# The third dense block's products in another order, and a head's norm spread half a piece later

## The chip, the cores and the metric

One core of a Trainium2 chip runs the whole program. The metric is the device time of one execution in microseconds. TensorE (PE) multiplies into PSUM banks of 128x512 floats; VectorE (DVE) and ScalarE (ACT) work on SBUF and PSUM; GpSimd (POOL) adds a little and issues transfers, SyncE (SP) issues most of them. Each engine runs its own instructions in program order and waits at semaphores for the others.

## The reference, cut to what matters

```python
for i in range(DEPTH):                       # two layers: gMLP mixer, then retention mixer
    h = rmsnorm(x, norm_mix_g[i])
    h = chunked_spatial_gating(h, ...) if i % 2 == 0 else retention(h, ...)
    x = x + h
    h = rmsnorm(x, norm_ffn_g[i])
    a = jax.nn.relu(h @ mlp_w1[i])           # 512 tokens x 4096 features
    x = x + (a * a) @ mlp_w2[i]
return rmsnorm(x, final_norm_g)
# retention, per head: o = rmsnorm(o, head_norm_g) * silu(g);  then  o @ w_out
```

The dense part of each layer and the head norm of the retention layer are what the change touches.

## The kernel before, in words

Every float32 product is three matmuls of float32r halves (`mm3`, L261): high by high, high by low, low by high. A weight piece is cast to its high half by ScalarE (L220) and its low half is taken by VectorE (L227, `tensor_sub`). The order of work is a list of steps written by hand; each step has one or two weight pieces. After a step's matmuls are issued, `refill` (L246) casts high halves up to three pieces ahead and takes low halves up to two pieces ahead. Matmuls of 512 columns go 24 to a piece (12 in each half of a product below).

**Dense layers.** `dense(l, hooks)` (L800) computes 4096 features in four groups of 1024: an up piece is 24 matmuls in a `mis` bank, and its evacuation is L695 (VectorE) and L696 (ScalarE). The second matrix product of the first three groups (blocks q = 0, 1, 2) is done by `seven(l, q)` (L719) with seven products of half-sized blocks, S0 to S6, in place of eight. Each product multiplies an operand of activations (`make(s)`: sums or differences of blocks by VectorE, their high halves by ScalarE in L763, their low halves by VectorE in L764) with a weight or a sum of weights. Operand s + 1 is made behind the first of product s's two pieces. `BANK = "acbacaa"` says which pair of PSUM banks (a, b or c) each product accumulates in: S0, S3, S5 and S6 use a, S1 and S4 use c, S2 uses b. After each product VectorE adds the pair's running sums to the token rows (L792), so the next product in the same pair waits for that.

The products alternate with up pieces, by a string of u and p. In blocks 0 and 1 every product is followed by an up piece. In the third block (q = 2) the string is `upupupupuupuupp`: its last two products stand next to each other. Just before the sixth product a `do` splits four chunks of activations of the last group into halves (`split_a`, L713 on ScalarE, L714 on VectorE), and four more behind it. Then comes the last quarter of the second matrix: in layer 0 `dn0` pieces (`down_last`, L836), in layer 1 `dt` pieces.

**Weights of the products.** Weight sums are formed by transfers: S5's weight is a load by SP (L165) followed by an accumulating load by POOL (L199, the add) into the same buffer, W12 + W22. S4's weight is W22 alone, a plain load. S1, S3 and S6 share one buffer to which further adds are applied once the earlier sum has been split. Loads take one of three rotating buffers as they come free, in the order of the steps.

**The head norm.** In the retention layer `o_unit(h)` (L1001) is the output product of head h: four pieces, each with two halves t of 12 matmuls, evacuated by L560. `finish_head(h + 1)` (L1010) hangs the next head's norm behind the pieces of `o_unit(h)`: behind piece 0 the sum of squares over the partitions, the reciprocal root and the two diagonal matrices `dg` (L340); behind piece 1 the two matmuls with ones that spread the row (`bc_h`, L344 and L345) and ScalarE's copy of it to SBUF (L346); behind pieces 2 and 3 `make_y` (L974 to L977), which scales the head and splits it into `ryH` and `ryL`. This is done for heads 1, 2 and 3; the third time, the product of head 3 follows at once and reads these halves. Head 0 has its norm elsewhere.

Of the kernel before, what the change touches and what calls it, by code (L numbers as in the profile page):

```python
# [88 lines left out]
def trunk(ctx, tc, x, norm_mix_g, norm_ffn_g, a_w_in, a_b_in, a_v_norm_g, a_w_s, a_b_s, a_w_out,  # L89
# [13 lines left out]
    def big(shape, dt, name):  # L103
        return bigp.tile(shape, dt, tag="big", name=name)

    def tmp(name, tag, bufs=2):
        return work.tile([P, T], F32, tag=tag, name=name, bufs=bufs)
# [7 lines left out]
    def acc(name):  # L115
        return psum.tile([P, 512], F32, tag="acc", name=name, bufs=6)
# [4 lines left out]
    def f32(ap):  # L121
        return ap.bitcast(F32)
# [110 lines left out]
    def launch(g):  # L233
        if next(g, "end") != "end":
            pending.append(g)

    def advance():
        for g in list(pending):
            if next(g, "end") == "end":
                pending.remove(g)  # L240
# [5 lines left out]
    def refill():  # L246
        n = pos["done"]
        prep(n + (LOOK if n >= 4 else 1), n + (LOOK - 1 if n >= 4 else 1))

    def step(fn, *ps):  # L250
        for p in ps:
            order.append(p)
            raws.extend(r for r in p.raws if r not in raws)
            for r in p.raws:
                r.uses += 1
        steps.append((fn, ps))
# [4 lines left out]
    def mm3(ps, ah, al, bh, bl, start, stop, resumed=False):  # L261

        for i, (a, b) in enumerate(((ah, bh), (ah, bl), (al, bh))):
            nc.tensor.matmul(ps, lhsT=a, rhs=b, start=start and i == 0, stop=stop and i == 2, skip_group_check=resumed)  # L264
# [96 lines left out]
    def mm_o(p, t, ps, bH, bL):  # L361
        ts = slice(t * P, (t + 1) * P)
        for k in range(4):
            mm3(ps, p.hi[:, k, ts], p.lo[:, k, ts], bH[:, k, :], bL[:, k, :], k == 0, k == 3)
# [187 lines left out]
    def evac_x(gcol=None, scaled=False):  # L552

        def ev(i, ps):
            if scaled:
                t = tmp(f"xs{i}", "uz")
                nc.vector.tensor_mul(t, ps, r2bc)
                nc.vector.tensor_add(xT[i], xT[i], t)
            else:
                nc.vector.tensor_add(xT[i], xT[i], ps)  # L560
            if gcol is not None:
                norm_chunk(i, gcol)
        return ev

    def out_piece(p, i, h, name, gcol=None, before=None, behind=None, act=None, bank=acc, scaled=False):

        ev = evac_x(gcol, scaled)
        hi, lo = act or (yH, yL)

        def run(p):  # L570
            if before:
                before()
            for t in range(2):
                ps = bank(f"{name}{h}_{i}{t}")
                mm_o(p, t, ps, hi[h], lo[h])
                if t == 1:
                    advance()
                    refill()
                    if behind:
                        behind()  # L580
                ev(2 * i + t, ps)
        step(run, p)

    def nxt(g, times=1):
        return lambda: [next(g, None) for _ in range(times)]
# [133 lines left out]
    def seven(l, q):  # L719

        w = mlp_w2[l]

        def part(i, j):
            r, c = 1024 * q + 512 * i, 512 * j
            return w[r : r + 512, c : c + 512].rearrange("(k p) n -> p k n", p=P)

        t1 = Raw(part(0, 0), adds=[part(0, 1)])
        t2 = Raw(part(1, 1), adds=[part(1, 1)], over=t1)
        t4 = Raw(part(1, 0), adds=[part(1, 0)], over=t2)
        wraws = [Raw(part(0, 0)), t1, Raw(part(1, 0)), t2, Raw(part(1, 1)), Raw(part(0, 1), adds=[part(1, 1)]), t4]  # L730
        pl = [[Piece(r, (slice(None), slice(2 * i, 2 * i + 2), slice(None)), [P, 2, 512]) for i in range(2)] for r in wraws]
        lo_t, hi_t = slice(0, T // 2), slice(T // 2, T)
        sums, parts, banks = {}, {}, {}

        def block(h, ts, c):
            return aF[2 * q + h][:, 2 * c : 2 * c + 2, ts]

        def half(v):
            return v.rearrange("p (k t) -> p k t", t=T // 2)

        def make(s):

            def src(c):
                if s in (0, 2, 6):
                    return block(*((0, lo_t), None, (1, lo_t), None, None, None, (1, hi_t))[s], c)
                if s == 1:
                    sums["s", c] = half(tmp(f"sa{l}{q}{c}", "uz"))
                    nc.vector.tensor_sub(out=sums["s", c], in0=block(0, hi_t, c), in1=block(1, hi_t, c))
                elif s == 3:
                    nc.vector.tensor_sub(out=sums["s", c], in0=sums["s", c], in1=block(0, lo_t, c))  # L750
                elif s == 4:
                    nc.vector.tensor_add(out=sums["s", c], in0=sums["s", c], in1=block(1, lo_t, c))
                else:
                    sums["d", c] = half(tmp(f"sd{l}{q}{c}", "sq"))
                    nc.vector.tensor_sub(out=sums["d", c], in0=block(0, lo_t, c), in1=block(0, hi_t, c))
                    return sums["d", c]
                return sums["s", c]

            sp = parts[s] = big([P, 2, 4, T // 2], F32R, f"sp{l}{q}{s}")
            for c in range(2):  # L760
                v = src(c)
                hi, lo = sp[:, 0, 2 * c : 2 * c + 2, :], sp[:, 1, 2 * c : 2 * c + 2, :]
                nc.scalar.copy(out=hi, in_=v)  # L763
                nc.vector.tensor_sub(out=lo, in0=v, in1=f32(hi))  # L764

        BANK = "acbacaa"
        FIRST = (0, 1, 2)
        OUT = [((0, 0), ALU.add), ((1, 1), ALU.add), ((0, 0), ALU.add), ((0, 1), ALU.subtract), ((0, 1), ALU.add), ((1, 1), ALU.subtract), ((1, 0), ALU.add)]

        def one(s, i):  # L770
            def run(p):
                bk = BANK[s]
                if i == 0 and s in FIRST:
                    banks[bk] = [acc(f"sm{l}{q}{bk}{t}") for t in range(2)]
                sp = parts[s]
                for t in range(2):
                    ts = slice(t * P, (t + 1) * P)
                    for k in range(2):
                        kk = 2 * i + k
                        mm3(banks[bk][t], sp[:, 0, kk, ts], sp[:, 1, kk, ts], p.hi[:, k, :], p.lo[:, k, :], s in FIRST and kk == 0, kk == 3, True)  # L780
                advance()
                refill()
                if i == 0 and s < 6:
                    make(s + 1)
                if i == 1:
                    (m, n), op = OUT[s]
                    for t in range(2):
                        v = tok[n][:, 2 * m + t, :]
                        if (n, m) in fresh:
                            nc.scalar.activation(v, banks[bk][t], AF.Copy, scale=1.0 if op == ALU.add else -1.0)  # L790
                        else:
                            nc.vector.tensor_tensor(out=v, in0=v, in1=banks[bk][t], op=op)  # L792
                    fresh.discard((n, m))
            return run

        return (lambda: make(0)), [lambda s=s: [step(one(s, i), pl[s][i]) for i in range(2)] for s in range(7)]

    fresh = set()

# [167 lines left out]
    def make_y(h, cs):  # L967
        if 0 in cs:
            yH[h] = big([P, 4, T], F32R, f"ryH{h}")
            yL[h] = big([P, 4, T], F32R, f"ryL{h}")  # L970

        def gen():
            for c in cs:
                nc.vector.tensor_mul(oo[h][:, c, :], oo[h][:, c, :], r2bc)  # L974
                nc.scalar.copy(out=yH[h][:, c, :], in_=oo[h][:, c, :])
            for c in cs:
                nc.vector.tensor_sub(out=yL[h][:, c, :], in0=oo[h][:, c, :], in1=f32(yH[h][:, c, :]))  # L977
            return
            yield
        launch(gen())  # L980
# [20 lines left out]
    def o_unit(h, gcol=None, behind=None):  # L1001
        behind = behind or {}
        pl = pieces_o(b_w_out[0], (h * DV, (h + 1) * DV), (0, D))
        for i in range(4):
            out_piece(pl[i], i, h, "ro", gcol, behind=behind.get(i))

    def each(fn, h):
        return {i: (lambda i=i: fn(h, i)) for i in range(4)}

    def finish_head(h):  # L1010
        g = head_norm(h)
        return {0: nxt(g, 3), 1: nxt(g), 2: lambda: make_y(h, (0, 1)), 3: lambda: make_y(h, (2, 3))}

    v_unit(0, {0: nxt(nrm1), 1: nxt(nrm1, 2), 3: nxt(nrm1)})
    do(trig_scaled)
# [123 lines left out]
    for k in range(2):  # L1139
        p = order[0]  # L1140
# [52 lines left out]
```

## Time and profile before

| | us |
|---|---|
| median of 3 runs | 1388.99 |
| lowest and highest run | 1388.95, 1390.54 |
| the profiled execution | 1390.09 |
| its span, first to last instruction | 1388.40 |
| TensorE busy in the span | 1367.0 (98%) |
| VectorE busy | 878.3 (63%) |
| ScalarE busy | 567.8 (41%) |
| mean granted TensorE clock | 0.994 |

A timeline row gives the start and the length in us, the engine (a q behind it means its queue), the line of the kernel, the operation, written and read tiles, shapes, how many instructions were merged in the row, and in brackets how long the engine sat idle before it and what ended that. A matmul's length counts its way through the pipeline; the next one starts before its end.

### The profile page before, as it was taken

The numbers are of one execution on the slowest core, as the hardware profiler recorded it, in microseconds if no ns is written. First come the engines' busy times: TensorE is split into PE (matmuls) and PEld (weight loads), VectorE is DVE, ScalarE is ACT, GpSimd is POOL, SyncE is SP. The second block draws the span as 40 slices with busy tenths as digits, with TensorE's granted clock in tenths as the row PEclk, the third lists the DMA queues.
The fourth block names the chain that finished last, engine by engine and source line by source line (L and its number), as shares of the span: only waits on it lengthen the run. The fifth ranks groups of instructions, "written<-read, shape, count | busy, mean of one in ns | idle before, by whom it ended". The sixth has DMA issues, their size and how long they took to land.

```text
span 1388.4 us, 15488 instructions
## 1 busy us (share of the span) xinstructions
PE 1367.0 (98%) x6180; PEld 1134.7 (82%) x6180; DVE 878.3 (63%) x1228; ACT 567.8 (41%) x812; POOL 158.0 (11%) x122
## 2 busy tenths in 40 slices
PE   9999999999999999999999999999999999999997
PEld 7888888888888888788888888888888888888875
DVE  7757756666656766676656574574594576657555
ACT  4646634234544443422333332323334444444342
POOL 3010111130100100021111100100121000100002
PEclk9999999999999999999999999999999999999999
DMA  6332222245665754623222222131137475765611
GB/s 229 110 117 81 75 89 92 91 144 155 148 191 152 183 144 130 165 84 99 84 70 81 70 95 87 61 122 61 61 95 209 93 187 175 152 182 152 172 56 61
DMA packets 115801, 166.71 MB, mean 120 GB/s; under 512 B 2881, under 2 KB 67985, under 8 KB 115473
## 3 DMA queue, kind: packets, MB, share of 16 engines
q1 hardware_dynamic: 103024, 140.55, 30.5%
q0 software_dynamic: 12672, 25.17, 10.7%
q8 instruction: 48, 0.79, 0.2%
q14 instruction: 25, 0.20, 0.0%
q10 hardware_dynamic: 32, 0.01, 0.0%
HBM read 163.62 MB, written 2.10 MB: 119 GB/s over the span
## 4 chain that ended last, share of the span: by engine, by line
PE 95%; DVE 3%; POOL 0%; ACT 0%; issue 0%; DMA 0%; SPq 0%; ACTq 0%; DVEq 0%
PE up L264 24%; PE g L264 6%; PE vv L264 6%; PE qk L264 6%; PE u L264 6%; PE o L264 6%; PE v L264 5%; PE ro L264 5%; PE dt L264 3%; PE dn L264 2%; PE av L264 2%; PE sm11a L264 2%; PE sm10a L264 2%; PE sm01a L264 2%; PE sm00a L264 2%; PE sm02a L264 2%
## 5 line engine op out<-in xcount | busy, mean ns | idle before, releaser
L227 DVE TENSOR_TENSOR wL<-raw,wH 128x1024 fp32r<-128x1024 f32 x235 | 300.6, 1282 | 56.1 <-issue 17.9
L220 ACT CAST wH<-raw 128x1024 fp32r<-128x1024 f32 x235 | 244.4, 1046 | 87.5 <-PE dt L264 13.1
L264 PE MATMUL up<-hH,wH 128*128 128x512 f32 x480 | 187.2, 390 | 0.2 <-ACT xtok L1038 0.2
L264 PE MATMUL up<-hL,wH 128*128 128x512 f32 x480 | 186.8, 389 | 0.0
L264 PE MATMUL up<-hH,wL 128*128 128x512 f32 x480 | 186.8, 389 | 0.0
L696 ACT ACTIVATE aF<-r 128x512 f32<-128x512 f32 x54 | 34.2, 633 | 207.7 <-DVE r L695 207.7
L695 DVE SCALAR_TENSOR_TENSOR r<-up,wide 128x512 f32<-128x512 f32 x54 | 37.3, 691 | 126.3 <-PE up L264 117.8
L264 PEld LDWEIGHTS up<-hH,wH 128*128 128x128 f32 x480 | 90.1, 188 | 19.0 <-ACT xtok L1038 0.5
L264 PEld LDWEIGHTS up<-hH,wL 128*128 128x128 f32 x480 | 90.1, 188 | 18.9
L264 PEld LDWEIGHTS up<-hL,wH 128*128 128x128 f32 x480 | 90.1, 188 | 18.7
L199 POOL DMA_DIRECT2D raw<-in_mlp_w_dram x22 | 29.0, 1366 | 421.5 <-DVE wL L227 257.1
L293 POOL TENSOR_TENSOR ssq<-ssq,sq 128x512 f32<-128x512 f32 x28 | 43.0, 1536 | 149.9 <-ACT sq L292 149.6
L227 DVE TENSOR_TENSOR wL<-more,wH 128x1024 fp32r<-128x1024 f32 x40 | 48.7, 1218 | 7.9 <-issue 6.4
L264 PE MATMUL u<-hH,wH 128*128 128x512 f32 x128 | 50.6, 395 | 0.0
L264 PE MATMUL g<-hH,wH 128*128 128x512 f32 x128 | 50.5, 395 | 0.0
L264 PE MATMUL o<-yH,wH 128*128 128x512 f32 x128 | 50.4, 394 | 0.0
L220 ACT CAST wH<-more 128x1024 fp32r<-128x1024 f32 x40 | 41.9, 1047 | 20.7 <-PE sm02a L264 6.5
L264 PE MATMUL qk<-hH,wH 128*128 128x512 f32 x128 | 50.0, 391 | 0.0
L264 PE MATMUL vv<-wH,hH 128*128 128x512 f32 x128 | 50.0, 391 | 0.0
L264 PE MATMUL ro<-ryH,wH 128*128 128x512 f32 x128 | 50.0, 391 | 0.0
L264 PE MATMUL ro<-ryH,wL 128*128 128x512 f32 x128 | 49.9, 390 | 0.0
L264 PE MATMUL vv<-wL,hH 128*128 128x512 f32 x128 | 49.9, 390 | 0.0
(394 smaller groups left out, 3101.9 us busy)
## 6 DMA issues: line engine op xcount, KB each, us to landing
raw<-in_mlp_w_dram SPq DMA_DIRECT2D x50, 1024.0 KB, 5.2
raw<-in_b_w_in_dram SPq DMA_DIRECT2D x24, 1024.0 KB, 5.0
raw<-in_mlp_w_dram POOLq DMA_DIRECT2D x22, 1024.0 KB, 9.3
more<-in_mlp_w_dram SPq DMA_DIRECT2D x20, 1024.0 KB, 5.4
raw<-in_a_w_in_dram SPq DMA_DIRECT2D x14, 1024.0 KB, 5.1
raw<-in_a_w_out_dram SPq DMA_DIRECT2D x8, 1024.0 KB, 5.0
raw<-in_b_w_out_dram SPq DMA_DIRECT2D x8, 1024.0 KB, 4.9
raw<-in_a_w_in_dram SPq DMA_DIRECT2D x8, 256.0 KB, 6.1
```

Of the source, the lines that this page charges most:

```text
L199: nc.gpsimd.dma_start(out=r.tile, in_=src, accum_op=ALU.add)
L220: nc.scalar.copy(out=p.hi, in_=p.src)
L227: nc.vector.tensor_sub(out=p.lo, in0=p.src, in1=f32(p.hi))
L264: nc.tensor.matmul(ps, lhsT=a, rhs=b, start=start and i == 0, stop=stop and i == 2, skip_group_check=resumed)
L293: nc.gpsimd.tensor_tensor(out=state["ssq"], in0=state["ssq"], in1=sq, op=ALU.add)
L695: nc.vector.scalar_tensor_tensor(out=r, in0=ps, scalar=0.0, in1=rbc, op0=ALU.max, op1=ALU.mult)
L696: nc.scalar.activation(a, r, AF.Square)
```

## The change

In the third block of either dense layer the products run in the order S0, S1, S2, S3, S5, S4, S6 (`PLAN`); an operand is still made one product ahead of its use, and the weights are loaded in the new order. The places of the products in the string of u and p stay. In the head norm of heads 1, 2 and 3 the spreading matmuls and the copy hang between the two halves of piece 2 of the output product, where they hung behind piece 1. The argument `before` of `out_piece`, which nobody used, is replaced by `between`.

```diff
-    def out_piece(p, i, h, name, gcol=None, before=None, behind=None, act=None, bank=acc, scaled=False):
+    def out_piece(p, i, h, name, gcol=None, between=None, behind=None, act=None, bank=acc, scaled=False):
         def run(p):
-            if before:
-                before()
             for t in range(2):
                 ps = bank(f"{name}{h}_{i}{t}")
                 mm_o(p, t, ps, hi[h], lo[h])
                 if t == 1:
                     advance()
                     refill()
                     if behind:
                         behind()
+                elif between:
+                    between()
                 ev(2 * i + t, ps)
...
+        PLAN = (0, 1, 2, 3, 5, 4, 6) if q == 2 else range(7)
         def one(s, i):
+            after = dict(zip(PLAN, PLAN[1:])).get(s)
...
-                if i == 0 and s < 6:
-                    make(s + 1)
+                if i == 0 and after is not None:
+                    make(after)
...
-        return (lambda: make(0)), [lambda s=s: [step(one(s, i), pl[s][i]) for i in range(2)] for s in range(7)]
+        return (lambda: make(0)), [lambda s=s: [step(one(s, i), pl[s][i]) for i in range(2)] for s in PLAN]
...
-            out_piece(pl[i], i, h, "ro", gcol, behind=behind.get(i))
+            out_piece(pl[i], i, h, "ro", gcol, between=behind.get((i, 0)), behind=behind.get(i))
...
-        return {0: nxt(g, 3), 1: nxt(g), 2: lambda: make_y(h, (0, 1)), 3: lambda: make_y(h, (2, 3))}
+        return {0: nxt(g, 3), (2, 0): nxt(g), 2: lambda: make_y(h, (0, 1)), 3: lambda: make_y(h, (2, 3))}
```

## Rows read from the trace of the kernel before

**Rows 1.** The page's busy table: busy us, share of the span, instructions.
```profile
PE 1367.0 (98%) x6180; PEld 1134.7 (82%) x6180; DVE 878.3 (63%) x1228; ACT 567.8 (41%) x812; POOL 158.0 (11%) x122
```
**Rows 2.** TensorE's waits, whole span: who, for whom, us, times, longest us.
```profile
PE sm02a L264 <- DVE ytok L792: 3.2, 1, 3.2
PE bc_h L344 <- DVE dg_h L340: 0.9, 3, 0.3
```
**Rows 3.** TensorE's timeline, layer 0, from S6's first matmul into dn0.
```profile
578.18 0.76 PE L264 MATMUL sm02a<-wH,sp 128*128 128x512 f32 x1 [3.21 <-DVE ytok L792]
...
586.31 0.39 PE L264 MATMUL dn0a<-aH,wH 128*128 128x512 f32 x1
...
586.76 0.39 PE L264 MATMUL dn0a<-aH,wL 128*128 128x512 f32 x1
```
**Rows 4.** Windows: us, busy us (count) by engine, granted clock, DMA share, GB/s.
```profile
578.00:583.00 5.00, 4.82 (x11) 3.80 (x12) 4.17 (x7) 0.96 (x2) 0.00 (x0) 0.50 0.00 0
1327.90:1331.20 3.30, 3.30 (x10) 2.53 (x9) 3.30 (x5) 0.14 (x1) 0.00 (x0) 0.50 0.00 0
31.50:33.50 2.00, 1.14 (x6) 0.90 (x6) 1.51 (x2) 0.46 (x1) 0.86 (x1) 1.00 0.00 0
```
**Rows 5.** TensorE's timeline, layer 1, S6's first matmul and dt's second.
```profile
1327.25 0.47 PE L264 MATMUL sm12a<-wH,sp 128*128 128x512 f32 x1 [3.22 <-DVE xtok L792]
...
1334.62 0.39 PE L264 MATMUL dt<-wL,aH 128*128 128x512 f32 x1
```
**Rows 6.** TensorE's timeline around head 3's spreading matmuls: the matmul before, the one behind.
```profile
1001.66 0.39 PE L264 MATMUL ro<-ryH,wL 128*128 128x512 f32 x1
...
1003.19 0.39 PE L264 MATMUL ro<-ryH,wH 128*128 128x512 f32 x1
```
**Rows 7.** VectorE's timeline, layer 0, from the activations' low halves to dn0's weight.
```profile
571.46 2.50 DVE L714 TENSOR_TENSOR aL<-aF,aH 128x512 fp32r<-128x512 f32 x4 [1.21 <-ACT aH L713]
...
575.01 1.28 DVE L764 TENSOR_TENSOR sp<-aF,sp 128x512 fp32r<-128x512 f32 x2
...
577.36 1.27 DVE L792 TENSOR_TENSOR ytok<-ytok,sm02a 128x512 f32<-128x512 f32 x2
...
580.96 1.21 DVE L227 TENSOR_TENSOR wL<-raw,wH 128x1024 fp32r<-128x1024 f32 x1
```
**Rows 8.** VectorE's timeline, layer 1, S6's operand and dt's first weight.
```profile
1324.09 1.29 DVE L764 TENSOR_TENSOR sp<-aF,sp 128x512 fp32r<-128x512 f32 x2
...
1330.03 1.22 DVE L227 TENSOR_TENSOR wL<-raw,wH 128x1024 fp32r<-128x1024 f32 x1
```
**Rows 9.** Timelines of SP, ScalarE and TensorE, layer 0, around the fifth product's weight.
```profile
522.80 0.37 SPq L165 DMA_DIRECT2D raw<-in_mlp_w_dram  x1
...
541.89 2.00 ACT L220 CAST wH<-raw 128x1024 fp32r<-128x1024 f32 x2
...
553.04 0.39 PE L264 MATMUL sm02c<-wH,sp 128*128 128x512 f32 x1
...
561.95 2.01 ACT L220 CAST wH<-raw 128x1024 fp32r<-128x1024 f32 x2 [3.64 <-DMA raw<-in_mlp_w_dram]
```
**Rows 10.** The page's loads by SP (median landing); landings of POOL's adds, line 199.
```profile
raw<-in_mlp_w_dram SPq DMA_DIRECT2D x50, 1024.0 KB, 5.2
...
DMA to landing us min/median/max: 8.4/9.0/17.5
```
**Rows 11.** Timelines of VectorE and ScalarE, head 3, behind the two diagonal matrices.
```profile
1001.51 1.29 DVE L340 TENSOR_TENSOR dg_h<-ident,sp_h 128x512 fp32r<-128x512 f32 x2
...
1003.38 0.59 ACT L346 COPY wide<-bc_h 128x512 f32<-128x512 f32 x1 [1.04 <-PE bc_h L345]
...
1007.98 1.28 DVE L974 TENSOR_TENSOR o<-o,wide 128x512 f32<-128x512 f32 x2
...
1011.57 0.69 DVE L560 TENSOR_TENSOR xT<-xT,ro 128x512 f32<-128x512 f32 x1 [0.33 <-PE ro L264]
...
1014.68 1.30 DVE L977 TENSOR_TENSOR ryL<-o,ryH 128x512 fp32r<-128x512 f32 x2
```

## The prediction

> **What bounds the kernel now.** I read the page's busy table first, then TensorE's waits, then the timelines around the two waits that the change touches. The busy table leaves TensorE 1367.0 of 1388.4 us, and VectorE, the next, 878.3 [rows 1]: only what TensorE loses can be won, and it loses little. Its waits name three places that this change touches: 3.2 us at `sm02a`, released by VectorE line 792, its twin in the second layer, `sm12a`, and 0.9 us in three waits at `bc_h`, released by line 340 [rows 2]. The reader should see that the first two belong to one spot, in either layer: the third block's last two products, S5 and S6, stand next to each other and both accumulate in bank a. S6's first matmul may not write it before VectorE has added S5's sum to the tokens (L792).
>
> The wait is larger than its row. The matmul before it would be followed after one pitch, 0.227 us (two matmuls lie 0.45 us apart [rows 3]), not after its full 0.39 us, so S6 starts 3.21 + 0.16 = 3.37 us late and would have begun at 574.81 instead of 578.18. Then TensorE works at half its clock: the granted clock is 0.50 (1.2 of 2.4 GHz) in the stretch behind each wait, where TensorE had stood idle just before. In a stretch near the kernel's start, where TensorE was idle for nearly 0.9 of 2 us, it stayed at 1.00 [rows 4]. S6's 24 matmuls should take 5.44 us; they take 586.31 - 578.18 = 8.13 in layer 0, 2.69 more. In layer 1 the dt phase begins one pitch before 1334.62, at 1334.39, so S6 takes 7.14 us, 1.70 more, behind a late start of 3.38 [rows 5]. Together 6.06 + 5.08 = 11.1 us are lost at this spot.
>
> At `bc_h` three steps (a product's last matmul and two spreading matmuls) take 1003.19 - 1001.66 = 1.53 us where three pitches are 0.68: 0.85 lost [rows 6], and the other two heads look the same. All that can be won is 11.1 + 2.55 = 13.7 us.
>
> **The change, part by part.** *S4 between S5 and S6.* S4 uses bank c, so S6 no longer stands right behind a user of its bank: the wait for L792 is gone. What is late next? VectorE, in its own program order. From 571.46 on it works without a break: four low halves of the activations, a weight's low half, S6's operand halves (L764, from 575.01), another weight, the evacuation of the product in front of S6 (L792), four low halves more, and the low half of dn0's first weight, 580.96 to 582.17 [rows 7]. This queue starts from the end of the last up piece, not from S5 or S6, and after the change it holds the same instructions in the same order, as make(6) stays one product ahead. So I keep its times. S6's third matmul needs the first L764, done near 575.70, and would be due at 574.81 + 0.45 = 575.26: with 0.1 us for the handover, 0.54 late. S6 then ends at 574.81 + 0.54 + 5.44 = 580.79. dn0's third matmul needs the weight that is ready at 582.17, so it starts at 582.27, about 1.0 late, against 586.76 before [rows 3]. Layer 0 wins 4.49 us.
>
> In layer 1 S6 nominally starts at 1327.25 - 3.38 = 1323.87; L764 makes it about 0.52 late; it ends at 1329.83. The dt phase's second matmul needs the low half that runs from 1330.03 to 1331.25 [rows 8] and starts at 1331.35, against 1334.62: 3.27 won. Idle stretches of 0.5 to 1.3 us are left, so I keep the clock at 1.00, as behind the short wait [rows 4].
>
> The moved product also moves its loads. S5's weight is a load by SP plus an accumulating load by POOL; it now takes the place in the queues that S4 had, one product earlier, and S4 takes S5's. SP then issues S5's load at 522.80 [rows 9]; such a load lands after 5.2 us [rows 10], so POOL issues its add near 528.5. The first cast from it is due on ScalarE at 541.89, and S5 must start near 553.04 [rows 9]. The 24 adds of this kind take 8.4, 9.0 and at worst 17.5 us to land [rows 10]: landing between 537 and 546. The late end would hold ScalarE 4 us, but the cast, the low half (1.22) and the matmul then still come before 553, so the cost is nothing, with 4 us left at the worst. S6's add follows on POOL, and it is earlier than before too; ScalarE's wait for S5's add (3.64 us before 561.95 [rows 9]) ends, but TensorE did not wait for that. S4's plain load takes S5's old place on SP and lands long before its use. SP and POOL carry the same transfers, in as many bytes. make(5) and make(4) change places: two subtractions and two additions of the same size, both ahead of their product as before. Cost nothing, covered by the product that runs meanwhile.
>
> *The spread half a piece later.* The two spreading matmuls move behind the first half of the next piece, 12 matmuls or 2.72 us later. dg is ready at 1001.51 + 1.29 = 1002.80, and the matmuls are now due near 1004.6: the wait goes, with about 0.04 left for the two joints, 0.81 won for each of three heads. Behind them in order waits ScalarE's copy of the row (0.59 us), now done near 1005.9 instead of 1003.97. Queued behind that copy on ScalarE is one weight cast that is needed three pieces later; the first user of the copy, L974, stands at 1007.98, kept there by VectorE's own queue [rows 11]. So 2 us of cover remain and the copy costs nothing. For heads 1 and 2 the output product is followed by query and key pieces, which need nothing of y: 0.81 each. For head 3, its own output product follows at once and needs the last low halves (L977 from 1014.68, first one ready near 1015.37). That product's start moves from 1014.07 (48 pitches behind 1003.19) to 1013.26, VectorE gains only what it had waited for TensorE, 0.33 plus the overlap, about 0.41 [rows 11]. So the low half comes at 14.96 + 0.1, where the eighth matmul is due at 14.85: 0.2 given back, 0.61 won. Bounds for this part are 0 (the row's wait returns elsewhere) and 2.55.
>
> **Sum.** 4.49 + 3.27 + 0.81 + 0.81 + 0.61 = 9.99 us. The profiled execution took 1390.09 us around its span of 1388.40; it would take 1380.10 around 1378.41. The median of the runs is 1388.99, 1.1 below the profiled one, so I forecast 1379.0 us, -0.72%. By bounds: at most 13.7 (1375.3), if VectorE's queue shortens too; the norm's part alone gives 1386.8.
>
> **Rivals.** *The clock falls all the same, or S6 is held longer.* The wait shrinks but VectorE's full queue still leaves TensorE idle around S6; were S6 held until L792 begins, 577.36 [rows 7], dn0 would start about 1 us later than I say in either layer (1381), and with the half clock over S6 as in the rows (2.69 + 1.70) the time is about 1383.4. For it speaks that the leftover idles lie within a few us of each other; against it, that VectorE's order gives S6's first operands early and that the short wait at the start left the clock at 1.00 [rows 4]. Chance 0.12. The Trainium skill ("TensorE: Matmul & The Clock Gate", section Why this matters for your kernels) warns that idle stretches between bursts send the clock back to half; the rows behind the long waits agree, and by it this rival hangs on how the leftover idle falls.
>
> *The order of products doesn't remove the wait.* If S6 still stopped for something that ends when L792 does, 11.1 us stay and only the norm's 2.2 us are won: 1386.8, within 0.2%. Against it: the row names L792 alone, and S6's other inputs are ready earlier in the queue [rows 2, 7]. Chance 0.05.
>
> *Slower: S5's add lands too late.* S5's weight now has to be there a product earlier. It decides from a landing at about 550: then cast, low half and product start behind 553.04, and every us later is lost in each layer. If the add came no sooner than it did, so that its cast stayed at 561.95 [rows 9], S5 would start near 564.3, 11 us late, in both layers: 1379.0 + 22 = 1401. For it: the add is the slowest transfer of the block. Against it: the buffer is freed at 522.80, and 550 would need an add of over 21 us, where the longest of 24 took 17.5 [rows 10]. Chance 0.04. The Trainium skill ("SBUF — State Buffer", section SBUF: two separate sides) says that a transfer issued by GpSimd can stand still while VectorE holds a port that both share, and VectorE is at work around 528; no row here shows an add that stood still beyond those times, so I only keep the rival from being nil on that account.
>
> **How the numbers follow.** Forecast 0.79, clock or longer hold 0.12, wait not removed 0.05, late add 0.04. The forecast itself spreads over some 1377 to 1381 (0.5 us for each handover, a little for the runs' own spread); to hold 8 in 10 with the clock rival, and a shorter VectorE queue at the low end, the range goes from 1376.3 to 1383.5. A difference of 0.2%, 2.8 us, is about what a measurement of this kernel can tell from no change. Forecast and first rival are faster by more: 0.90, a little less than their sum; within 0.2%: 0.06; slower: 0.04.
>
> **What would show it.** Right: no TensorE wait for L792 in the third blocks, S6 starting within 1 us of the product in front of it, about 1 us idle at the start of dn0 and of dt released by VectorE L227, granted clock 1.00 there, and at `bc_h` no wait. Wrong: a ScalarE wait for an accumulating load before S5 of more than 8 us; a clock of 0.50 near S6; a new wait of the last output product for ryL of over 0.5 us.

## The result, and the profile after

The changed kernel took 1381.11 us (median of 4 runs, 1380.43 to 1382.22) against 1388.97 us for the kernel before (4 runs, 1387.84 to 1390.54): 0.9943 of it, with an interval of 0.9926 to 0.9961, or 7.9 us less. It is faster, and it lies within the range; it is 2.1 us above the forecast of 1379.0. The profiled execution of the changed kernel took 1382.22 us around a span of 1380.5 us.

Lines from 770 on have moved by four: L792 is now L796, L974 is L978 and L977 is L981.

The busy table answers [rows 1]. TensorE is busy 3.5 us less with the same 6180 matmuls: fewer of them ran at the lower clock. The rest of the gain is idle time.

```profile
PE 1363.5 (99%) x6180; PEld 1132.1 (82%) x6180; DVE 877.5 (64%) x1228; ACT 567.3 (41%) x812; POOL 158.0 (11%) x122
```

All of TensorE's waits after the change (who, line, for whom; us in total, times, longest). They answer [rows 2]:

```profile
PE xt L452 <- DVE hL L459: 2.2, 1, 2.2
PE warm L1140 <- POOL ident masks.py:199: 1.4, 1, 1.4
PE dt L264 <- DVE wL L227: 0.9, 1, 0.9
PE st_mix L326 <- POOL st_mix L317: 0.9, 1, 0.9
PE dn0a L264 <- DVE wL L227: 0.7, 1, 0.7
PE up L264 <- ACT xtok L1042: 0.2, 1, 0.2
```

The rows for `sm02a`, `sm12a` and `bc_h` are gone. Two new ones stand at the places that the prediction named, the starts of `dn0` and of `dt`, and both are released by VectorE's low halves of weights (L227), not by the evacuation. `xt`, `warm` and `st_mix` belong to the start of the kernel, which the change does not touch.

TensorE's timeline in layer 0, from the end of S4 through S6 into `dn0` (start, length). It answers [rows 3]:

```profile
576.40 0.39 PE L264 MATMUL sm02c<-wH,sp 128*128 128x512 f32 x1
576.63 0.39 PE L264 MATMUL sm02a<-wH,sp 128*128 128x512 f32 x1
576.98 0.50 PE L264 MATMUL sm02a<-wL,sp 128*128 128x512 f32 x1
577.58 0.73 PE L264 MATMUL sm02a<-wH,sp 128*128 128x512 f32 x2
...
582.47 0.39 PE L264 MATMUL sm02a<-wH,sp 128*128 128x512 f32 x1
582.70 0.39 PE L264 MATMUL dn0a<-aH,wH 128*128 128x512 f32 x1
582.93 0.39 PE L264 MATMUL dn0a<-aL,wH 128*128 128x512 f32 x1
584.05 0.50 PE L264 MATMUL dn0a<-aH,wL 128*128 128x512 f32 x1 [0.74 <-DVE wL L227]
```

S6 now follows S4 after one pitch (576.40 to 576.63); it hesitates twice in its first three matmuls, and then runs through at 0.227 us each. From its first matmul to `dn0`'s first are 6.07 us where 24 pitches are 5.44: 0.6 lost, where the kernel before lost 6.1 at this spot. `dn0`'s third matmul comes 584.05 - 582.70 = 1.35 us behind its first where two pitches are 0.45: 0.9 late.

VectorE's queue over the same stretch shows what TensorE now waits for, and answers [rows 7]:

```profile
573.29 2.50 DVE L714 TENSOR_TENSOR aL<-aF,aH 128x512 fp32r<-128x512 f32 x4 [1.21 <-ACT aH L713]
575.70 1.22 DVE L227 TENSOR_TENSOR wL<-raw,wH 128x1024 fp32r<-128x1024 f32 x1
576.84 1.28 DVE L764 TENSOR_TENSOR sp<-aF,sp 128x512 fp32r<-128x512 f32 x2
578.04 1.22 DVE L227 TENSOR_TENSOR wL<-raw,wH 128x1024 fp32r<-128x1024 f32 x1
579.18 1.28 DVE L796 TENSOR_TENSOR ytok<-ytok,sm02c 128x512 f32<-128x512 f32 x2
580.38 2.49 DVE L714 TENSOR_TENSOR aL<-aF,aH 128x512 fp32r<-128x512 f32 x4
582.79 2.35 DVE L227 TENSOR_TENSOR wL<-raw,wH 128x1024 fp32r<-128x1024 f32 x2
```

It is the queue of before, instruction for instruction, with the start 1.83 us later: L714 at 573.29 for 571.46, the evacuation at 579.18 for 577.36, `dn0`'s weight at 582.79 for 580.96. Only what TensorE needs from it is another thing. S6's second matmul (576.98) follows the weight's low half that ends at 576.92, its third (577.58) the first half of L764, near 577.48. The evacuation at 579.18 is now that of bank c, and nobody waits for it.

In layer 1, TensorE from S6 into `dt` (answers [rows 5]):

```profile
1319.15 0.39 PE L264 MATMUL sm12a<-wH,sp 128*128 128x512 f32 x1
...
1325.04 0.39 PE L264 MATMUL sm12a<-wH,sp 128*128 128x512 f32 x1
...
1326.58 0.50 PE L264 MATMUL dt<-wL,aH 128*128 128x512 f32 x1 [0.93 <-DVE wL L227]
```

The clock over both spots (windows: us, busy us and count by engine, granted clock, DMA share, GB/s), to be held against [rows 4]:

```profile
574.00:578.00 4.00, 3.90 (x17) 2.73 (x16) 4.00 (x6) 4.00 (x7) 0.00 (x0) 1.00 0.00 0
578.00:583.00 5.00, 5.00 (x24) 4.05 (x22) 5.00 (x9) 3.81 (x7) 0.00 (x0) 1.00 0.00 0
583.00:590.00 7.00, 6.26 (x28) 4.95 (x27) 4.47 (x5) 0.99 (x1) 0.00 (x0) 1.00 0.54 177
1318.00:1323.00 5.00, 4.89 (x21) 3.49 (x19) 5.00 (x8) 5.00 (x9) 0.00 (x0) 1.00 0.01 2
1323.00:1328.00 5.00, 4.07 (x18) 3.08 (x17) 5.00 (x7) 2.31 (x3) 0.00 (x0) 1.00 0.00 0
```

1.00 everywhere, where the row of before for 578 to 583 reads 0.50.

S5's weight, in the queue place that the change gives it: timelines of SP (its load), POOL (the add) and ScalarE (the two casts from it). They answer [rows 9], and the landing times behind them [rows 10]:

```profile
524.63 0.37 SPq L165 DMA_DIRECT2D raw<-in_mlp_w_dram  x1
...
530.09 1.28 POOL L199 DMA_DIRECT2D raw<-in_mlp_w_dram  x1 [13.15 <-DVE wL L227]
...
543.72 2.00 ACT L220 CAST wH<-raw 128x1024 fp32r<-128x1024 f32 x2
```

The view of line 199 gives the landing times of the 24 adds:

```profile
DMA to landing us min/median/max: 8.6/9.0/12.9
```

The casts have no wait in brackets. The view of the transfers issued between 529 and 536 us gives 10.7 us for this add, so it landed near 540.8. Even the slowest add of this execution, 12.9 us, would have landed at 543.0, ahead of 543.72.

Head 3's spreading matmuls on TensorE, the copy on ScalarE and its first reader on VectorE (answer [rows 6] and [rows 11]):

```profile
1000.19 0.40 PE L264 MATMUL ro<-ryH,wL 128*128 128x512 f32 x1
1000.42 0.40 PE L344 MATMUL bc_h<-dg_h,onesr 128*128 128x512 f32 x1
1000.66 0.40 PE L345 MATMUL bc_h<-dg_h,onesr 128*128 128x512 f32 x1
1000.90 0.40 PE L264 MATMUL ro<-ryH,wH 128*128 128x512 f32 x1
...
1001.10 0.59 ACT L346 COPY wide<-bc_h 128x512 f32<-128x512 f32 x1 [2.94 <-PE bc_h L345]
...
1003.79 1.29 DVE L978 TENSOR_TENSOR o<-o,wide 128x512 f32<-128x512 f32 x2
```

Three steps now take 1000.90 - 1000.19 = 0.71 us, three pitches with 0.03 for the joints, where they took 1.53. The copy ends at 1001.69, 2.1 us ahead of the instruction that reads it.

### Where the time went

Start-to-start times of TensorE's stages, each from one first matmul to the next, of the profiled executions (us). "Third block" runs from S0's first matmul to `dn0`'s or `dt`'s first, and includes the up pieces between the products; 336 matmuls at one pitch would take 76.16. The start runs from the beginning of the span to `v`'s first matmul of L264, the tail from `dt`'s last matmul to the end of the span.

| kernel | start | third block, layer 0 | `dn0` | to the next up pieces, with retention | third block, layer 1 | `dt` | tail |
|---|---|---|---|---|---|---|---|
| before | 35.53 | 82.23 | 47.25 | 402.29 | 81.23 | 43.29 | 10.69 |
| after | 37.36 | 76.79 | 48.28 | 400.14 | 76.83 | 44.52 | 10.70 |
| order only | 35.82 | 76.79 | 48.31 | 402.28 | 76.77 | 44.59 | 10.70 |
| norm only | 36.04 | 81.17 | 47.25 | 400.15 | 81.27 | 43.29 | 10.70 |
| old order, late splits | 37.11 | 77.05 | 47.25 | 402.30 | 77.03 | 43.29 | 10.97 |
| change, late splits | 35.84 | 76.16 | 47.25 | 400.15 | 76.16 | 43.29 | 10.99 |
| change, one late split | 35.80 | 76.83 | 47.25 | 400.14 | 76.83 | 43.29 | 10.70 |
| spread behind the piece | 37.26 | 76.79 | 48.28 | 400.81 | 76.79 | 44.55 | 10.69 |
| before, again | 36.24 | 82.27 | 47.25 | 402.28 | 81.23 | 43.29 | 10.68 |
| after, again | 36.29 | 76.79 | 48.32 | 400.18 | 76.83 | 44.51 | 10.70 |

The stages left out (468.53 to 468.57 and 217.31) are the same in all. The stages that the change does not touch repeat to within 0.05 us, except the start, which is 35.5 to 37.4 us whatever the kernel, and the tail of the two kernels with both groups of splits later. From before to after, layer 0 wins (82.23 + 47.25) - (76.79 + 48.28) = 4.41 us, layer 1 (81.23 + 43.29) - (76.83 + 44.52) = 3.17, and the norm 2.15: 9.73 us in all. The profiled span is only 7.9 us shorter because its start was 1.83 us longer.

### The profile page after: what moved, and what is told of

It is laid out like the page before. It is cut to its first block, busy times and chain, and to the rows that moved or that the text cites. A ratio compares the mean times of both kernels' runs of the same rounds, so it can differ in the third digit from the quotient of the medians.

```text
span 1380.5 us, 15485 instructions
## 1 busy us (share of the span) xinstructions
PE 1363.5 (99%) x6180; PEld 1132.1 (82%) x6180; DVE 877.5 (64%) x1228; ACT 567.3 (41%) x812; POOL 158.0 (11%) x122
## 4 chain that ended last, share of the span: by engine, by line
PE 96%; DVE 2%; POOL 1%; ACT 0%; issue 0%; DVEq 0%; POOLq 0%; ACTq 0%
PE up L264 24%; PE g L264 6%; PE ro L264 6%; PE vv L264 6%; PE qk L264 6%; PE u L264 6%; PE o L264 6%; PE v L264 5%; PE dt L264 3%; PE dn L264 2%; PE av L264 2%; PE sm11a L264 2%; PE sm10a L264 2%; PE sm01a L264 2%; PE sm00a L264 2%; PE sm12a L264 1%
## 5 line engine op out<-in xcount | busy, mean ns | idle before, releaser
L227 DVE TENSOR_TENSOR wL<-raw,wH 128x1024 fp32r<-128x1024 f32 x235 | 300.5, 1283 | 48.9 <-issue 13.8
L264 PE MATMUL up<-hH,wH 128*128 128x512 f32 x480 | 187.2, 390 | 0.2 <-ACT xtok L1042 0.2
L264 PE MATMUL up<-hL,wH 128*128 128x512 f32 x480 | 186.8, 389 | 0.0
L264 PE MATMUL up<-hH,wL 128*128 128x512 f32 x480 | 186.8, 389 | 0.0
L695 DVE SCALAR_TENSOR_TENSOR r<-up,wide 128x512 f32<-128x512 f32 x54 | 37.4, 692 | 128.5 <-PE up L264 120.0
L264 PEld LDWEIGHTS up<-hH,wH 128*128 128x128 f32 x480 | 90.1, 188 | 19.1 <-ACT xtok L1042 0.5
L264 PEld LDWEIGHTS up<-hH,wL 128*128 128x128 f32 x480 | 90.1, 188 | 18.8
L264 PEld LDWEIGHTS up<-hL,wH 128*128 128x128 f32 x480 | 90.1, 188 | 18.7
L227 DVE TENSOR_TENSOR wL<-more,wH 128x1024 fp32r<-128x1024 f32 x40 | 48.7, 1219 | 6.2 <-issue 4.7
L264 PE MATMUL u<-hH,wH 128*128 128x512 f32 x128 | 50.6, 395 | 0.0
L264 PE MATMUL g<-hH,wH 128*128 128x512 f32 x128 | 50.5, 395 | 0.0
L264 PE MATMUL o<-yH,wH 128*128 128x512 f32 x128 | 50.4, 394 | 0.0
L264 PE MATMUL ro<-ryL,wH 128*128 128x512 f32 x128 | 50.0, 391 | 0.0
L264 PE MATMUL qk<-hH,wH 128*128 128x512 f32 x128 | 50.0, 391 | 0.0
L264 PE MATMUL vv<-wH,hH 128*128 128x512 f32 x128 | 50.0, 391 | 0.0
L264 PE MATMUL ro<-ryH,wH 128*128 128x512 f32 x128 | 50.0, 390 | 0.0
L264 PE MATMUL ro<-ryH,wL 128*128 128x512 f32 x128 | 50.0, 390 | 0.0
L264 PE MATMUL g<-hH,wL 128*128 128x512 f32 x128 | 49.9, 390 | 0.0
```

Source lines behind the costliest of these rows:

```text
L227: nc.vector.tensor_sub(out=p.lo, in0=p.src, in1=f32(p.hi))
L695: nc.vector.scalar_tensor_tensor(out=r, in0=ps, scalar=0.0, in1=rbc, op0=ALU.max, op1=ALU.mult)
```

## The experiments

The theory: VectorE's queue is the same before and after; the old order made S6 wait for the evacuation, which stands late in that queue, and the new one makes S6 wait only for its operands, which stand earlier. The half clock was a consequence of the long wait, and the norm's part is separate. The rivals: that the two parts help or hinder each other; that the shared bank itself, not the queue, made the wait; that the clock or chance between runs made the difference.

**Order only.** The norm goes back to its old place.

```diff
-        return {0: nxt(g, 3), (2, 0): nxt(g), 2: ..., 3: ...}
+        return {0: nxt(g, 3), 1: nxt(g), 2: ..., 3: ...}
```

> The products' order alone; the norm's spread stays behind piece 1. My theory (S6 waited for S5's sum in the shared bank, and VectorE's queue sets what is left): 7.8 us below the kernel before; S6 starts about 0.6 us late, dn0 and dt wait about 1.0 and 1.2 us for their first weight's low half, granted clock 1.00 around them; the three spreads still lose 0.85 us each. Rival (the gain came from elsewhere, such as the norm or the loads that moved): clearly less than 7.

Measured: 1382.38 us (1381.43 to 1382.84) against 1389.17 for the kernel before (15 runs, 1386.29 to 1391.45); 0.9952 of it, 0.994 to 0.9965. Its row at the spreading matmuls is that of [rows 2] again:

```profile
PE bc_h L344 <- DVE dg_h L340: 0.9, 3, 0.3
```

The two layers win 4.38 and 3.16 us by the stage table, as in the full change, and the retention stage wins nothing. The medians differ by 6.8 us where 7.8 were expected, and where less than 7 was to speak for the rival; it is the stages, which win 7.54 without the norm, that speak against it. Of the 15 runs of the kernel before, 9 have a mean clock of 0.996, above the 0.994 of its profile, and so had less to win (below, *Before again*).

**Norm only.** The products go back to their old order.

```diff
-        PLAN = (0, 1, 2, 3, 5, 4, 6) if q == 2 else range(7)
+        PLAN = range(7)
```

> The spread half a piece later alone; products in the old order. My theory: 2.2 us below the kernel before (0.81 + 0.81 + 0.61), no wait at the spreading matmuls, some 0.2 us given back at the start of head 3's output product; S6's waits of 3.2 us and the half clock behind them stay. Rival (the wait moves to the users of the spread row): no difference, and VectorE's L974 waits for ScalarE's copy.

Measured: 1387.44 us (11 runs, 1382.83 to 1389.42), 0.9984 of the kernel before, 0.9972 to 0.9996. Its TensorE waits hold both S6 rows and no `bc_h`:

```profile
PE sm12a L264 <- DVE xtok L796: 3.2, 1, 3.2
PE sm02a L264 <- DVE ytok L796: 3.2, 1, 3.2
```

The medians differ by 1.7 us (2.2 expected); the retention stage wins 2.14 us. So the parts add up: 4.38 + 3.16 + 2.14 = 9.68, and the full change wins 9.73. But in layer 0 S6 loses less to the clock here than in the profile of before (TensorE's timeline, and the window as above):

```profile
578.68 0.77 PE L264 MATMUL sm02a<-wH,sp 128*128 128x512 f32 x1 [3.21 <-DVE ytok L796]
...
585.75 0.39 PE L264 MATMUL dn0a<-aH,wH 128*128 128x512 f32 x1
```

```profile
578.00:583.00 5.00, 4.32 (x12) 3.47 (x13) 4.67 (x7) 1.46 (x2) 0.00 (x0) 0.66 0.00 0
```

Behind the same wait of 3.2 us the mean of this window is 0.66 for 0.50: the half clock ended earlier. S6 took 585.75 - 578.68 = 7.07 us and lost 1.63 of them to it, not 2.69. In layer 1 it took 7.18 and lost 1.74, as before (1.70). The runs of this kernel spread over 6.6 us, and their mean granted clocks with them: 0.998 in the three quickest (1382.83, 1383.97 and 1384.23 us), 0.993 to 0.995 in the others. No other kernel here spreads so far.

**Old order, splits later.** From the kernel before, with neither part of the change: the four low halves that stand ahead of S5 go behind it, and the four behind S5 go behind S6. VectorE then has no low halves of activations between S5 and its evacuation.

```diff
                     if q == 2 and j == 6:
+                        do(lambda: [split_a(l, i) for i in range(4)])
+                    if q == 2 and j == 7:
                         do(lambda: [split_a(l, i) for i in range(4, 8)])
...
-                    if q == 2 and i == 8:
-                        do(lambda: [split_a(l, i) for i in range(4)])
```

> Products in the old order and the old norm, but the two groups of four splits of activations are moved: the first from in front of S5 to behind it, the second from behind S5 to behind S6. S5's sum is then taken from the bank as soon as TensorE has made it. If the wait's cost was mostly VectorE's queue ahead of the evacuation (rival to the bank alone as the cause), S6 starts some 1.1 us late in place of 3.4, the clock stays at 1.00, dn0 and dt don't wait, and the time is about 9 us below the kernel before, though S5 and S6 still share a bank. If sharing the bank by itself costs the 3.4 us and the half clock, the time stays where it was, within 1 us.

Measured: 1381.56 us (1380.86 to 1382.56), 0.9949 of the kernel before, 0.9936 to 0.9961. S5 and S6 still stand next to each other in bank a, and S6 still waits for the evacuation, but for 0.6 us in place of 3.2, at the full clock. Its TensorE waits in the third blocks:

```profile
PE sm02a L264 <- DVE ytok L792: 0.6, 1, 0.6
PE sm12a L264 <- DVE xtok L792: 0.6, 1, 0.6
```

VectorE's timeline, the evacuation that S6 waits for and what now follows it:

```profile
576.31 1.27 DVE L792 TENSOR_TENSOR ytok<-ytok,sm02a 128x512 f32<-128x512 f32 x2
577.50 2.49 DVE L714 TENSOR_TENSOR aL<-aF,aH 128x512 fp32r<-128x512 f32 x4
```

The window behind the wait:

```profile
578.00:583.00 5.00, 5.00 (x24) 4.13 (x23) 4.99 (x8) 3.28 (x6) 0.00 (x0) 1.00 0.00 0
```

The shared bank gave the wait its place, but the work ahead of the evacuation gave it its length: without the splits (2.5 us of low halves on VectorE, behind their casts on ScalarE) 2.6 of the 3.2 us are gone. S6 starts 577.13 - 576.35 = 0.8 us late, where 1.1 was expected. What is left still looks like VectorE's queue: by the kernel's order TensorE is done with the first of S5's two banks after the 18th of its 24 matmuls, by an estimate from the pitch near 575.2 (S5 begins at 570.91), and VectorE reaches L792 at 576.31, with no idle time before it. No run here has S6's bank shared and nothing ahead of the evacuation. The layers win 5.18 and 4.20 us this way, more than the change's 4.41 and 3.17, since `dn0` and `dt` lose nothing. The medians differ by 7.6 us where about 9 were expected; they do not tell this kernel (1381.56) from the order alone (1382.38).

**The change, splits later.** The same move made in the changed kernel.

> The changed kernel with the splits moved as in the run above. If VectorE's queue (low halves ahead of S6's operand and of dn0's weight) is what is late behind the change, the 0.6 us at S6 and the 1.0 and 1.2 us at dn0 and dt go too: some 2.8 to 3.4 us below the changed kernel, 11 to 13 below the kernel before, and no wait of TensorE for VectorE in the third blocks. If something else holds TensorE there, no more than 1 us is won against the changed kernel.

Measured: 1377.47 us (1377.13 to 1378.3), 0.992 of the kernel before, 0.9907 to 0.9934. No wait is left in the third blocks, and both stages take the 76.16 us of their 336 matmuls. TensorE over both spots:

```profile
560.00:590.00 30.00, 30.00 (x134) 24.86 (x133) 20.53 (x27) 13.80 (x20) 0.00 (x0) 1.00 0.45 158
1310.00:1340.00 30.00, 30.00 (x134) 24.82 (x134) 19.82 (x25) 13.86 (x20) 0.00 (x0) 1.00 0.20 74
```

It is the quickest of these kernels: its slowest run is 1 us below the quickest of the changed kernel (1379.34), and its median is 3.4 to 3.6 below that kernel's two medians. The order alone leaves 0.6 + 1.1 us in layer 0 and 0.6 + 1.3 in layer 1; the splits alone leave 0.9 in each; together they leave nothing.

**The change, one split later.** Only the second four low halves move, behind S6.

```diff
-                    if q == 2 and j == 6:
+                    if q == 2 and j == 7:
                         do(lambda: [split_a(l, i) for i in range(4, 8)])
```

> The changed kernel with only the second group of four splits moved, behind S6. Theory (these four low halves, 2.49 us on VectorE, hold back dn0's and dt's first weight): the waits at dn0 and dt go (1.0 and 1.2 us), the 0.6 us at S6 stay, as the first group still runs ahead of S6's operand. If the first group alone sets both, the waits at dn0 and dt stay.

Measured in a single run: 1378.4 us. The waits at `dn0` and `dt` are gone (47.25 and 43.29 us, as in the kernel before), and S6's 0.6 us in either layer stays. So each group of low halves has its own victim: the first delays S6's operands, the second the first weight of the phase behind S6.

**Spread behind the piece.** The spreading matmuls and the copy go another half piece later, behind piece 2, right ahead of the instructions that use the row.

```diff
-        return {0: nxt(g, 3), (2, 0): nxt(g), 2: lambda: make_y(h, (0, 1)), 3: ...}
+        return {0: nxt(g, 3), 2: lambda: (next(g, None), make_y(h, (0, 1))), 3: ...}
```

> The changed kernel with the spread moved another half piece, behind piece 2 of the output product and right in front of the first half of y. My theory (after the change the copy has 2 us of cover before VectorE's L974): another 2.7 us uses up the cover, L974 waits about 0.7 us for the copy, the spreading matmuls still lose nothing, and head 3's output product, which reads y at once, waits some 0.7 us longer for ryL; the retention stage is 0.5 to 1 us longer than the changed kernel's. Rival (the spread's place beyond the change costs nothing): the stage stays within 0.1 us.

Measured in a single run: 1382.76 us; the retention stage is 0.67 us longer than after the change (400.81). Head 3's output product now waits for VectorE, by TensorE's waits:

```profile
PE ro L264 <- DVE ryL L981: 0.2, 1, 0.2
```

and VectorE for the copy, by its timeline:

```profile
1004.36 1.29 DVE L978 TENSOR_TENSOR o<-o,wide 128x512 f32<-128x512 f32 x2 [0.58 <-ACT wide L346]
```

A delay of one half piece (2.72 us) uses up the 2.1 us of cover and 0.58 more, and TensorE loses 0.67 for it. The cover that the prediction put at 2 us was real, and it was not more than that.

**Before again, after again.** Both kernels unchanged, on one chip, to see how far they repeat.

> The kernel before once more, for its profile. The changed kernel's profiled execution took 1.8 us longer up to the end of the first v piece (37.4 against 35.5 us), ahead of all that the change touches. If that is chance of the execution, this start takes anything from 35 to 38 us, and the loss at the half clock behind S6 differs too (2.7 and 1.7 us in the first profile, 1.6 to 1.7 in another kernel with the old order). If it belongs to the changed program, this start is again within 0.3 us of 35.5. Every stage behind the start without a half clock repeats within 0.1 us.

> The changed kernel once more, for its profile. If the longer start was chance, it takes anything from 35 to 38 us; if it belongs to the changed program, it is again within 0.3 us of 37.4. Behind the start every stage as in its first profile within 0.1 us, clock 1.00 at S6; time about 8 to 10 us below the kernel before.

Measured: before 1387.88 us (12 runs, 1386.81 to 1390.87) against 1390.49 in the 17 runs beside it (1386.49 to 1392.21), a ratio of 0.9995, 0.9984 to 1.0006; after 1380.91 (6 runs, 1379.34 to 1381.21), 0.9933, 0.9919 to 0.9948. The stages of after repeat to 0.05 us apart from the start (36.29 for 37.36). The starts, 36.24 and 36.29, agree with each other and with neither of the first profiles (35.53 and 37.36), so the longer start of after was chance of the execution. The loss at S6, though, did not differ as was expected of chance: the third blocks of before took 82.27 and 81.23 us, as in its first profile (82.23 and 81.23). The runs of before fall in two groups that the mean granted clock tells apart. Of the 44 runs of this kernel taken with the experiments, 24 with a mean clock of 0.996 have a median of 1387.6 us, and 18 with 0.993 or 0.994 one of about 1390.8. Which group holds the middle run decides the median, which is why it can lie 2.6 us apart for one program where the ratio says no difference. The profile of before, at 0.994 and 1390.09 us, is of the second group; so is the profile taken here (1390.8 us).

## Why the prediction was right, and where it was off

**S4 between S5 and S6: right.** Forecast 4.49 and 3.27 us, measured 4.41 and 3.17. The step that carried it, that VectorE's queue keeps its order and its times, holds row by row with the start's shift of 1.83 us. What would be late next was named rightly: S6's third matmul by L764 (forecast 0.54 and 0.52 late, measured 0.50 in both layers; S6 as a whole loses 0.63 and 0.67), `dn0`'s third by the weight's low half (1.0 forecast, 0.90 measured; the stage is 1.03 longer), `dt`'s second by the same (1.3 forecast, 1.08 measured; the stage is 1.23 longer). One small thing was missed: S6's second matmul also waits, some 0.12 us, for its own weight's low half.

**S5's load and add: right.** The load is issued at 524.63 and the cast starts at 543.72, both exactly 1.83 us behind the forecast's 522.80 and 541.89; the add was issued 1.59 behind the 528.5 of the forecast, within that shift. The rival of a late add is refuted: ScalarE did not wait.

**The norm: right.** Forecast 0.81 + 0.81 + 0.61 = 2.23, measured 0.76 + 0.84 + 0.55 = 2.15 for heads 1, 2 and 3; head 3's product gives back 0.23 where 0.2 was forecast. The experiment that moves the spread further shows that the copy's cover was what kept it free.

**The wait is not removed: refuted** by the profile of after, and by the order-only run, which wins the two layers' gains without the norm. **The clock falls again: did not happen.** The granted clock is 1.00 at both spots after, with idle stretches of 0.1 to 0.9 us. The Trainium skill ("TensorE: Matmul & The Clock Gate", section Why this matters for your kernels) warns of idle stretches between bursts; the traces agree so far that the clock fell behind the idle 3.2 us of before and not behind these. That was less safe than the prediction took it to be: in the starts of norm only and of after again it fell behind a wait of 1.8 us (last section). The price of this rival in the prediction, 1383.4, was added up wrongly, as it puts the whole 2.69 + 1.70 us on top. By the same rows the half clock alone would have taken up the waits at `dn0` and `dt` and cost 1.7 + 0.4 us (about 1381.1); with S6 also held until L792 it would have cost 3.7 + 2.5 (about 1385.1), above the range.

**The base: the step that was off.** The stages came out 0.26 us short of the sum (9.73 for 9.99), and the start of the profiled execution was 1.83 us longer than in the profile of before: 1380.10 + 0.26 + 1.83 = 1382.19, where it took 1382.22. The last step of the sum, from the profile to the median, was forecast as 1.1 and measured as 1.11 (1382.22 to 1381.11). So the 2.1 us between the forecast and the median are the stages and the start. That the last step came out was luck, as far as the runs show, for in the two kernels it has different grounds:
- The profile of before was one of the second group, with 2.69 and 1.70 us lost to the half clock. Other runs of before lie below it at a higher mean clock: 0.002 more over 1388 us is 2.8 us, about the 3.2 between the groups' medians. The sum took the full 4.39 us away from the profile, and then 1.1 us more for the median. But the changed kernel has no half clock there in any of the six profiles with its order of products, so it has none of that to lose less of. So the 1.1 us look counted twice; this is argued from the mean clocks, which don't tell where in a run the clock was low.
- The start was 35.53 us in the profile of before, the shortest of the ten, and 37.36 and 36.29 in the two of the changed kernel, 1.83 and 0.76 above the forecast's base; in the repeat the step from the profile to the median is only 0.30 (1381.21 to 1380.91). The start holds no instruction that the change touches. TensorE's wait for the input's load in it is 0.9 to 1.9 us in the seven profiles that list it, and in three of the ten (norm only; old order, splits later; after again) the clock fell there too: the twelve matmuls of `v` ahead of its end took 4.3 us in place of 2.7 to 2.8.

With the start of the repeat, 0.76 in place of 1.83, the sum without its last step is 1381.12, where the repeat's profiled execution took 1381.21 and the first median is 1381.11. The range held because it had been opened for the clock and for VectorE's queue, not for these two.

**What stays open.** Why the half clock behind the same wait ends sooner in some executions, and whether it is missing altogether in the quickest: none of the three norm-only runs at a mean clock of 0.998 was the profiled one. For it speaks that the profile of after has the same mean clock, 0.998, and by its window no half clock before 1370 us, and by then every matmul has begun:

```profile
0.00:1370.00 1370.00, 1363.29 (x6180) 1132.13 (x6180) 871.57 (x1201) 564.39 (x807) 155.46 (x120) 1.00 0.42 121
```

Two of the three runs (1383.97 and 1384.23 us) also lie where the norm-only profile would without its losses at S6, 1387.44 - 1.63 - 1.74 = 1384.07. That VectorE's queue sets the wait's length is shown by the late splits; that more than half of the runs of before would win less from the change than its profile says follows from their mean clocks and is not seen in a trace of such a run. The tail of both kernels with two late splits is 0.3 us longer (10.97 and 10.99 for 10.70); the traces put it at one VectorE instruction (L1067, in the changed kernel L1071), which takes 1.13 us there and 0.83 to 0.84 in before, in after and with one late split, and do not say why.

## What to carry to other kernels

A wait for a shared bank has two parts, the bank and whatever stands ahead of the evacuation in the evacuating engine's queue. Here at least 2.6 of 3.2 us were the queue. Moving work that is not urgent behind the evacuation won more in these stages (9.4 us) than putting a product of another bank between did (7.5), and the two together won all that was lost there. When one wait is taken away, read the next late thing from the other engine's unchanged program order: it gave each of four new delays to about 0.2 us. When a gain includes a clock that fell, read the mean clock of several runs of the kernel before, and do not carry the difference between its profile and its median over to the changed kernel.

## What the runs showed of the hardware that was not expected

Waits of one length did not cost the same at the clock. Behind S6's wait of 3.2 us in layer 0 the granted clock of the window 578 to 583 was 0.50 (1.2 of 2.4 GHz) in the profile of before and 0.66 in that of norm only, and S6 lost 2.69 and 1.63 us. The two profiles of before itself agree (S6 took 8.13 and 8.17 us), so that it differs between executions of one program rests on their times and mean clocks: 1382.83 to 1389.42 us for norm only, at 0.998 to 0.993, and the two groups of before, at 0.996 and at 0.993 or 0.994.

The clock also fell in the start of three profiles, behind waits shorter than 3.2 us: TensorE's waits listed from 10 to 36 us are one of 1.8 us in norm only and in after again, and two of 0.7 and 0.9 in old order, splits later; the clock from 34 to 36 us was then 0.55, 0.50 and 0.50. In the first profile of after, the same program as after again, it stayed at 1.00. After again, behind a stretch where TensorE was busy 0.37 of 2 us, and then after, in the stretch where it was busy least:

```profile
30.00:32.00 2.00, 0.37 (x2) 0.33 (x3) 2.00 (x2) 0.24 (x1) 1.57 (x1) 1.00 0.00 0
32.00:34.00 2.00, 2.00 (x8) 1.58 (x7) 1.94 (x3) 0.00 (x0) 0.00 (x0) 0.66 0.21 32
34.00:36.00 2.00, 2.00 (x6) 1.60 (x5) 1.65 (x11) 0.00 (x0) 0.00 (x0) 0.50 0.92 266
```

```profile
32.00:34.00 2.00, 1.29 (x5) 0.52 (x3) 0.15 (x1) 1.57 (x2) 1.27 (x2) 1.00 0.00 0
```
